# A decoder block with a product-key expert layer on one core: nine list tiles a block in place of ten

## The chip, the cores and the metric

The kernel runs on one core of a Trainium2 chip. The metric is the device time of one execution in microseconds (us). Before the change the median of three runs is 1511.7 us (1509.28 to 1516.68).

## The reference

One decoder layer for 1024 tokens of width 1024: two mixing branches with an output projection, then an expert layer (PEER), then a final norm. All matrices are float32. What matters here is the expert layer:

```python
q = jnp.einsum('btd,dq->btq', h, w_q).reshape(B, T, H, 2, PEER_DQ // 2)
s1 = jnp.einsum('bthc,kc->bthk', q[..., 0, :], keys1)
s2 = jnp.einsum('bthc,kc->bthk', q[..., 1, :], keys2)
v1, i1 = lax.top_k(s1, K)          # K = 16, H = 8 heads, 128 keys
v2, i2 = lax.top_k(s2, K)
cand = (v1[..., :, None] + v2[..., None, :]).reshape(B, T, H, K * K)
cidx = (i1[..., :, None] * PEER_NKEYS + i2[..., None, :]).reshape(B, T, H, K * K)
top_s, pos = lax.top_k(cand, K)
idx = jnp.take_along_axis(cidx, pos, axis=-1)
g = jax.nn.softmax(top_s, axis=-1)
...
u = expert_down[ii]
a = jax.nn.gelu(jnp.einsum('pd,ped->pe', xx, u), approximate=False)
vv = expert_up[ii]
return jnp.einsum('pe,ped->pd', gg * a, vv)
```

Each token picks 16 of 16384 experts in each of 8 heads. The scores are large (the inputs scale the query weights and both key tables by 8), so most of the 16 softmax gates underflow to zero in float32.

## The kernel before, in words

The 1024 tokens are handled as two halves of 512 and eight blocks of 128 (blocks 0 to 3 and 4 to 7). For each half a chain of weight groups is streamed (`stream`, L1180): a 128x512 weight tile is loaded by SP, split into a high and a low float32r part by ScalarE (L1190) and VectorE (L1191), and multiplied in three passes (L178 to L186). The last groups of a half are the output projection (`w_out_part`) and the four query groups `w_q(0)` to `w_q(3)`. After each of those, `s_part` computes the key scores, `tops` takes the best 8 (L197, L198), and `rank(q)` writes the expert indices of each token's best expert for two heads into a table (L1548).

**Directs and lists.** For each token and head the best expert always counts. These eight "direct" tiles a block (128 tokens, one head) are gathered by the index table, one 128x2048 row pair a token (or two gathers of 128x1024, where the buffer is a pair), dotted with the tokens (L518), and added with a diagonal weight matrix (L586, plain float32). The experts of rank 2 to 8 count only where their gate is at least the smallest normal float32. They are packed into one list a block. `pack_half` counts the entries of each block (`cnt`), and the list is processed in tiles of 128 entries: `peer_E` builds a one-hot matrix (L691, L692), `entry_list` moves the entries' indices and gates with two matmuls (L531, L532), gathers 128 rows of both expert tables (L509), and `entry_dot` fetches the tokens' activations with four matmuls (L561, L562) and dots them in two halves (L563). Blocks 0 and 1 gather the tokens' activations instead (L547) and dot them at once (L568). In the first stage the weighted rows are added in float32r with a split (L595, L596, then four matmuls at L603, L604); in the second stage in plain float32 (two matmuls at L586). The number of list tiles a block is the constant `NT` (L43); entries past the end of a list give tiles whose rows have weight zero, and they are gathered and added all the same.

Heads whose eighth gate is not zero (`flags`) leave the lists and go through one "rare" list for each half (`NTR`, six tiles each).

**The order.** `peer_stream` (L738) writes the order of all tiles out: the rare list of the first half, the lists of blocks 0 to 3 (their directs were summed earlier by `direct_rows`), some directs of blocks 5, 6, 7 and 4 (`EARLY`), and then, as a second stage with its own pools, the remaining directs (`LATER`), the lists of blocks 4 to 7, the second rare list, and the final rows. The first stage is pumped by `step()` in between the weight groups of the second half; directs are only listed once their `rank(q)` has been issued (`topped`). The buffers of gathered rows are used in a fixed ring (`RING`, `RING9`), and up to `AH` tiles are gathered ahead. A scheduler with a model of the machine then sets each engine's order, so that one constant can move many instructions.

**The general pass.** `peer_rest` (L898) adds up by how much each count exceeds its capacity, `caps` (L905, `NT * 128` entries a block). If the sum is above zero, a loop over all eight blocks and 128 selections each redoes the whole layer (L913 on). Otherwise it is skipped. It follows the last tile.

Of the kernel before, what the change touches and what calls it, by code (L numbers as in the profile page):

```python
# [39 lines left out]
GRP = {b: (g, i) for g, bs in enumerate(GROUPS) for i, b in enumerate(bs)}  # L40
ROW0 = (0, 16, 24, 32, 40, 44, 48, 52, 56)
NC_ = 64
NT = 10  # L43
NTR = (6, 6)
EB = 2
WS = 4
# [31 lines left out]
def block_kernel(ctx: ExitStack, tc: tile.TileContext, x, xT, cT, w_ada, b_ada, b_adaT, n1T, w_inp, w_alr,  # L78
# [37 lines left out]
    def load_const(name, src, shape, pool=None):  # L116
# [8 lines left out]

    ebase = const.tile([P, NT], F32, name="ebase")
    nc.gpsimd.iota(ebase, pattern=[[P, NT]], base=0, channel_multiplier=0,
                   allow_small_or_imprecise_dtypes=True)
# [350 lines left out]
    def load_block(pl, b, h2):  # L479
        hh = hl = None  # L480
        if pl["own"] or b not in HRB:
            if h2 is None:
                h2 = load_h2(b)
            ph = use[turns[0] % len(use)]["ph"]
            turns[0] += 1
            hh = ph.tile([P, D], F32R, name="hh", tag="hh")
            hl = ph.tile([P, D], F32R, name="hl", tag="hl")
            nc.scalar.activation(hh, h2, AF.Identity)
            nc.vector.tensor_tensor(hl, h2, hh.bitcast(F32), op=OP.subtract)
        if b in onchip:  # L490
            return b, hh, hl, *onchip[b]
        n = ncs_of[b]
        th = pl["pw"].tile([P, 3 * NCS + 2], F32R, name="thl")[:, :3 * n + 2]
        tl = pl["pw"].tile([P, 2 * NCS], F32R, name="tll")[:, :2 * n]
        nc.scalar.dma_start(th.bitcast(F32), ts_d[b][:, :3 * n + 2])
        nc.scalar.dma_start(tl.bitcast(F32), ts_d[b][:, 3 * n + 2:])
        return b, hh, hl, th, tl
# [177 lines left out]
    def peer_prep(pl, b, h2):  # L675
        blk = load_block(pl, b, h2)
        mid = pl["pw"].tile([P, NT], F32, name="mid")
        hw = pl["pw"].tile([P, 2], F32, name="hw")
# [6 lines left out]
    def peer_E(pl, pb, j):  # L685
        blk, mid, hw = pb
        eb = pl["eb"]
        n = min(eb, NT - j) * P
        ea = pl["pq"].tile([P, eb * P], F32, name="ea", bufs=1)
# [48 lines left out]
    def peer_stream():  # L738
        last = PH + NT
        todo, opens, closes, runs = [], set(), set(), set()  # L740
# [157 lines left out]
    def peer_rest(pl, pg_):  # L898
# [5 lines left out]
        morei = pc.tile([1, 1], I32, name="morei")  # L904
        caps = [NT * P] * NBLK + [t * P for t in NTR] + [P] * NG  # L905
        for i, c in enumerate(caps):
# [758 lines left out]
```

## Time and profile before

| | |
|---|---|
| median of 3 runs | 1511.7 us (1509.28 to 1516.68) |
| profiled execution: its own time | 1513.0 us |
| profiled execution: span of the trace | 1511.3 us |
| PE busy | 1386.3 us (92%) |
| VectorE (DVE) busy | 1116.6 us (74%) |
| ScalarE (ACT) busy | 751.4 us (50%) |
| GpSimd (POOL) busy | 331.5 us (22%) |
| moved by DMA | 360 MB, mean 238 GB/s |

The own time lies 1.7 us over the span. Busy time of PE is the sum of matmul records that overlap each other, so it can be close to the span without PE being at its peak. POOL issues all gathers, in order. The first stage of the expert tiles runs from about 795 us, beside the second half's weight groups, the hand-over to the second stage takes from about 1224 to 1345 us, and the second stage's lists run to the end.

### The profile page before, as it was taken

To read this page: it belongs to the slowest core of one execution; us is meant where nothing else is said; L and a number is where in the kernel's file an instruction comes from. 1 tells how busy PE (TensorE), PEld (TensorE's weight loads), DVE (VectorE), ACT (ScalarE), POOL (GpSimd) and SP (SyncE) were. 2 spreads that over 40 slices of the span, in tenths; PEclk is the share of its full clock that TensorE was granted. 3 is DMA by queue.
4 is the path that set the end of the run, shared out by engine and by line. 5 is a ranking of instruction groups with operands and counts; after the bars stand their busy time and mean duration, and the time that the engine had idled before them with its cause. 6 is when DMAs were issued, how large, how long until landed. Compare 5 with 4: busy or idle time off the path is not lost.

```text
span 1511.3 us, 20046 instructions
## 1 busy us (share of the span) xinstructions
PE 1386.3 (92%) x6076; PEld 1060.7 (70%) x6076; DVE 1116.6 (74%) x3189; ACT 751.4 (50%) x1659; POOL 331.5 (22%) x302
## 2 busy tenths in 40 slices
PE   3999999999997999989899999998989999679985
PEld 2778777888776877668677878876778775246542
DVE  6483867434567779987789678779898786898883
ACT  4463333332445545474445675556555555455542
POOL 0000002000000121602433132311111145554430
PEclk7899999999999999999999999999999999889998
DMA  9553644233358545856776698976878669899964
GB/s 317 182 198 103 202 147 140 98 105 118 132 196 281 197 162 175 299 185 206 257 264 238 217 349 312 343 267 226 299 285 278 247 263 360 332 406 390 356 252 149
DMA packets 126167, 360.24 MB, mean 238 GB/s; under 512 B 15625, under 2 KB 25097, under 8 KB 115170
## 3 DMA queue, kind: packets, MB, share of 16 engines
q0 software_dynamic: 35952, 175.39, 31.5%
q1 hardware_dynamic: 70272, 132.15, 25.8%
q10 hardware_dynamic: 19826, 51.34, 9.6%
q8 instruction: 49, 0.80, 0.2%
q14 instruction: 68, 0.56, 0.1%
HBM read 334.60 MB, written 24.23 MB: 237 GB/s over the span
## 4 chain that ended last, share of the span: by engine, by line
PE 61%; DMA 16%; DVE 15%; issue 4%; ACT 3%; POOL 1%; ACTq 0%; SPq 0%; DVEq 0%; POOLq 0%
PE mm L178 10%; PE mm L179 10%; PE mm L181 10%; PE acc L586 5%; PE mm L184 4%; PE mm L185 4%; PE mm L186 4%; DMA uv<-in_tab_dram,dix 3%; DMA uv<-in_tab_dram,ix 2%; DMA wada<-in_w_ada_dram 2%; DVE wl L1191 2%; PE hps L561 2%; PE hps L562 1%; DMA wt<-in_w_outp_dram 1%; DVE ti L198 1%
## 5 line engine op out<-in xcount | busy, mean ns | idle before, releaser
L1190 ACT ACTIVATE wh<-wt 128x512 fp32r<-128x512 f32 x368 | 228.3, 628 | 309.2 <-PE mm L179 115.9
L1191 DVE TENSOR_TENSOR wl<-wt,wh 128x512 fp32r<-128x512 f32 x368 | 248.9, 686 | 154.3 <-ACT wh L1190 81.0
L178 PE MATMUL mm<-wh,hTh 128*128 128x512 f32 x672 | 266.9, 399 | 2.3 <-ACT wh L1190 2.3
L179 PE MATMUL mm<-wh,hTl 128*128 128x512 f32 x672 | 265.9, 398 | 0.0
L181 PE MATMUL mm<-wl,hTh 128*128 128x512 f32 x672 | 209.2, 397 | 0.0
L178 PEld LDWEIGHTS mm<-wh,hTh 128*128 128x128 f32 x672 | 128.3, 191 | 34.8 <-ACT wh L1190 4.5
L179 PEld LDWEIGHTS mm<-wh,hTl 128*128 128x128 f32 x672 | 128.3, 191 | 27.9 <-issue 0.9
L181 PEld LDWEIGHTS mm<-wl,hTh 128*128 128x128 f32 x672 | 126.6, 189 | 28.0 <-DVE wl L1191 0.7
L509 POOL DMA_INDIRECT uv<-in_tab_dram,ix x70 | 78.2, 1118 | 274.6 <-ACT ix L540 135.9
L184 PE MATMUL mm<-wh,hTh 128*128 128x512 f32 x224 | 91.5, 417 | 15.6 <-ACT hTh L1144 6.4
L178 PE MATMUL mm<-hTh,wh 128*128 128x512 f32 x240 | 95.9, 400 | 0.0
L179 PE MATMUL mm<-hTl,wh 128*128 128x512 f32 x240 | 95.5, 398 | 0.0
L185 PE MATMUL mm<-wl,hTh 128*128 128x512 f32 x224 | 89.7, 400 | 0.0
L186 PE MATMUL mm<-wh,hTl 128*128 128x512 f32 x224 | 89.0, 400 | 0.0
L184 PE MATMUL mm<-hTh,wh 128*128 128x256 f32 (+1 forms) x208 | 72.1, 350 | 11.4 <-ACT vt L1235 5.5
L561 PE MATMUL hps<-hh,E 128*128 128x512 f32 x144 | 71.8, 500 | 11.0 <-DVE uv L563 8.9
L563 DVE SCALAR_TENSOR_TENSOR uv<-uv,hps 128x512 f32<-128x512 f32 x100 | 66.8, 682 | 17.9 <-PE hps L562 9.4
L181 PE MATMUL mm<-hTh,wl 128*128 128x512 f32 x240 | 74.0, 401 | 0.0
L185 PE MATMUL mm<-hTl,wh 128*128 128x256 f32 (+1 forms) x208 | 70.8, 342 | 2.5 <-DVE hTl L170 2.5
L596 DVE SCALAR_TENSOR_TENSOR vl<-uv,r,vh 128x512 fp32r<-128x512 f32 x88 | 63.7, 746 | 11.1 <-PE acc L604 5.9
L186 PE MATMUL mm<-hTh,wl 128*128 128x256 f32 (+1 forms) x208 | 69.8, 342 | 1.2 <-DVE wl L1191 1.0
L712 POOL DMA_INDIRECT uvd<-in_down_dram,dix x32 | 37.1, 1159 | 139.9 <-DVE ts L351 45.7
(977 smaller groups left out, 3021.0 us busy)
## 6 DMA issues: line engine op xcount, KB each, us to landing
wt<-in_w_inp_dram SPq DMA_DIRECT2D x224, 256.0 KB, 3.1
wt<-in_w_qp_dram SPq DMA_DIRECT2D x80, 256.0 KB, 3.2
wada<-in_w_ada_dram SPq DMA_DIRECT2D x32, 512.0 KB, 4.3
wt<-in_w_outp_dram SPq DMA_DIRECT2D x64, 256.0 KB, 3.6
wada<-in_w_ada_dram SPq DMA_DIRECT2D x32, 256.0 KB, 6.0
s_d<-so ACTq DMA_DIRECT2D x32, 256.0 KB, 3.5
h2l<-h_d ACTq DMA_DIRECT2D x13, 512.0 KB, 7.0
xr<-in_x_dram ACTq DMA_DIRECT2D x8, 512.0 KB
```

What stands on the lines that cost most here:

```text
L178: nc.tensor.matmul(ps, lh, rh, start=False, stop=False)
L179: nc.tensor.matmul(ps, *((lh, rl) if feat else (ll, rh)), start=False, stop=False)
L181: nc.tensor.matmul(ps, *((ll, rh) if feat else (lh, rl)), start=False, stop=False)
L184: nc.tensor.matmul(ps, lh, rh, start=first, stop=False)
L185: nc.tensor.matmul(ps, lh, rl, start=False, stop=False)
L186: return nc.tensor.matmul(ps, ll, rh, start=False, stop=last).ins
L509: nc.gpsimd.indirect_dma_start(out=dst[:], out_offset=None, in_=src, in_offset=off)
L561: nc.tensor.matmul(hps, Ej, hh[:, sl], start=True, stop=False)
L563: nc.vector.scalar_tensor_tensor(uv[0][:, sl], uv[0][:, sl], 1.0, hps, op0=OP.mult, op1=OP.mult, accum_out=r[:, 2 + n:3 + n])
L586: nc.tensor.matmul(acc[:, sl], W, v[:, sl], start=first, stop=last)
L1190: nc.scalar.activation(wh, wt, AF.Identity)
L1191: nc.vector.tensor_tensor(wl, wt, wh.bitcast(F32), op=OP.subtract)
```

## The change

The constant `NT` is 9 in place of 10, so that each block's list has nine tiles, 1152 entries of capacity in place of 1280, and blocks with more entries go through the general pass.

```diff
 NC_ = 64
-NT = 10
+NT = 9
 NTR = (6, 6)
```

Through `NT` it changes the width of `ebase` and `mid` (L126, L677), the last direct or list index `last` (L739), the width of the last one-hot matrix (L688) and `caps` (L905). PE's order is the same up to the first list tile of block 0, and differs from there on.

The first place is POOL's order at the hand-over from the lists of block 3 to the directs (`dix_0_136` and `dix_1_137` are the index tables that `rank(0)` and `rank(1)` of the second half write; `ix` is a list's index; `fs` belongs to the finish of a block). Before:

```order
L509 DMA uv<-in_tab_dram,ix 128x2048
L509 DMA uv<-in_tab_dram,dix_0_136 128x2048
L509 DMA uvu<-in_down_dram,ix 128x1024
L509 DMA uvv<-in_up_dram,ix 128x1024
L509 DMA uvu<-in_down_dram,dix_0_136 128x1024
L509 DMA uvv<-in_up_dram,dix_0_136 128x1024
L166 TENSOR_TENSOR fs<-fs,mhalf 128x1
L509 DMA uv<-in_tab_dram,dix_1_137 128x2048
```

After the change:

```order
L509 DMA uv<-in_tab_dram,ix 128x2048 x4
L509 DMA uvu<-in_down_dram,dix_0_136 128x1024
L509 DMA uvv<-in_up_dram,dix_0_136 128x1024
L509 DMA uv<-in_tab_dram,dix_0_136 128x2048 x2
L166 TENSOR_TENSOR fs<-fs,mhalf 128x1
L509 DMA uvu<-in_down_dram,dix_1_137 128x1024
L509 DMA uvv<-in_up_dram,dix_1_137 128x1024
```

All list gathers now stand ahead of the first direct gather, and three direct gathers in place of two stand ahead of block 3's finish.

The second place is VectorE's order ahead of `rank(3)` (L1548, `dix_3_139`), which frees the last quarter of the directs; L518 is the dot of one direct. Before:

```order
L518 SCALAR_TENSOR_TENSOR uvu,rd<-uvu,h2l 128x1024
L518 SCALAR_TENSOR_TENSOR uv,rd<-uv,h2l 128x1024
L198 MAX_INDEX ti<-tv,so 128x8 x6
L345 TENSOR_TENSOR cand<-tv 128x8x8
L345 TENSOR_TENSOR cand<-tv 128x8x4 x3
L1548 SCALAR_TENSOR_TENSOR dix_3_139<-ti 128x8
```

After the change:

```order
L198 MAX_INDEX ti<-tv,so 128x8 x4
L345 TENSOR_TENSOR cand<-tv 128x8x8
L345 TENSOR_TENSOR cand<-tv 128x8x4 x3
L518 SCALAR_TENSOR_TENSOR uv,rd<-uv,h2l 128x1024
L1548 SCALAR_TENSOR_TENSOR dix_3_139<-ti 128x8
```

One dot now stands directly ahead of the index write. Over the whole order 22 of the 32 direct dots stand ahead of it, where 20 did; in POOL's order 23 direct gathers stand ahead of the first that needs it, as before.

## Rows read from the trace of the kernel before

**Rows 1.** The page: span, and the chain that ended last, by engine.

```profile
span 1511.3 us, 20046 instructions
...
PE 61%; DMA 16%; DVE 15%; issue 4%; ACT 3%; POOL 1%; ACTq 0%; SPq 0%; DVEq 0%; POOLq 0%
```

**Rows 2.** Busy time by window: PE, PEld, DVE, ACT, POOL; PEclk; DMA share; GB/s.

```profile
795.00:900.00 105.00, 101.58 (x447) 82.43 (x446) 84.47 (x223) 66.48 (x155) 30.39 (x26) 0.98 0.74 262
900.00:1000.00 100.00, 97.43 (x463) 80.09 (x462) 78.03 (x200) 62.74 (x147) 28.20 (x25) 1.00 0.89 327
1000.00:1130.00 130.00, 116.47 (x520) 91.94 (x519) 112.52 (x260) 76.23 (x165) 19.34 (x18) 0.93 0.75 265
1130.00:1244.00 114.00, 109.40 (x570) 89.56 (x570) 93.06 (x356) 63.50 (x135) 30.04 (x27) 0.99 0.72 257
...
1350.00:1440.00 90.00, 88.93 (x302) 52.02 (x301) 73.46 (x309) 51.43 (x170) 40.93 (x42) 1.00 0.97 373
```

**Rows 3.** The chain that ended last, second stage: start, length, what.

```profile
1364.45 1.72 PE acc L586 x4
...
1367.55 1.72 PE acc L586 x4
...
1408.13 1.73 PE acc L586 x4
```

**Rows 4.** PE in order of time, one list tile of the second stage.

```profile
1390.71 1.88 PE L586 MATMUL acc<-uvv,W 128*128 128x512 f32 x4
1392.03 0.80 PE L561 MATMUL hps<-hh,E 128*128 128x512 f32 x1
1392.67 0.39 PE L562 MATMUL hps<-hl,E 128*128 128x512 f32 x1
1392.90 0.24 PE L531 MATMUL tps<-th,E 128*128 128x170 f32 x1
...
1393.60 1.88 PE L586 MATMUL acc<-uv,W 128*128 128x512 f32 x4
```

**Rows 5.** PE in order of time, a stretch of weight matmuls without expert tiles.

```profile
319.75 0.39 PE L185 MATMUL mm<-wl,hTh 128*128 128x512 f32 x1
...
322.93 0.39 PE L186 MATMUL mm<-wh,hTl 128*128 128x512 f32 x1
```

**Rows 6.** Groups of VectorE instructions, 795 to 1244 us: busy, mean ns, idle before.

```profile
L596 DVE SCALAR_TENSOR_TENSOR vl<-uv,r,vh 128x512 fp32r<-128x512 f32 x88 | 63.7, 746 | 11.1 <-PE acc L604 5.9 <-ACT vh L595 4.0 <-PE hps L562 0.7
L563 DVE SCALAR_TENSOR_TENSOR uv<-uv,hps 128x512 f32<-128x512 f32 x48 | 32.1, 681 | 10.5 <-DMA uv<-in_tab_dram,ix 8.1 <-PE hps L562 2.2
L568 DVE SCALAR_TENSOR_TENSOR uv<-uv,hr 128x1024 f32<-128x1024 f32 x20 | 24.4, 1221 | 12.6 <-DMA uv<-in_tab_dram,ix 9.4 <-DMA hr<-h_d,ix 3.3
L692 DVE TENSOR_SCALAR E<-ea,hw 128x128 fp32r<-128x128 f32 x44 | 12.4, 281 | 1.4 <-PE tps L532 1.1 <-ACT ea L691 0.4
L563 DVE DVE_READ_ACCUMULATOR uv<-uv,hps 128x1 f32 x48 | 3.9, 82 | 0.0
```

**Rows 7.** POOL in order of time at the hand-over, with the idle time before.

```profile
1193.32 0.95 POOL L509 DMA_INDIRECT uvv<-in_up_dram,dix  x1 [0.30 <-issue]
1222.21 0.56 POOL L166 TENSOR_TENSOR fs<-fs,mhalf 128x1 f32<-128x1 f32 x1 [27.95 <-DVE fs L165]
1223.94 1.45 POOL L509 DMA_INDIRECT uv<-in_tab_dram,dix  x1 [1.17 <-DVE dix L1548]
...
1300.45 0.94 POOL L509 DMA_INDIRECT uvu<-in_down_dram,dix  x1 [13.22 <-DVE ts L351]
```

**Rows 8.** Groups of PE instructions, 795 to 1244 us.

```profile
L604 PE MATMUL acc<-vl,e 128*128 128x512 f32 x92 | 38.2, 415 | 2.6 <-DVE vl L596 2.6
...
L561 PE MATMUL hps<-hh,E 128*128 128x512 f32 x52 | 21.9, 421 | 4.9 <-DVE uv L563 4.7 <-ACT ts__9424 L534 0.2
...
L531 PE MATMUL tps<-thl,E 128*128 128x170 f32 (+1 forms) x45 | 11.5, 258 | 1.1 <-DVE uv L563 1.1
```

**Rows 9.** The chain that ended last: a gather of the hand-over, and the last block's finish.

```profile
1239.74 12.95 DMA uv<-in_tab_dram,dix
...
1475.82 10.16 DMA yrv<-x_d
...
1494.27 3.71 PE acc L586 x8
```

## The prediction

> **What bounds the kernel now.** I read the page first. The chain that ended last lies 61% on PE, 16% on DMA and 15% on VectorE [rows 1], so no single engine's busy time gives the answer, and what a list tile is worth has to be read in each stage. The change removes eight list tiles, the tenth of each block: four in the first stage (blocks 0 to 3, beside the weight groups of the second half) and four in the second stage (blocks 4 to 7).
>
> The second view is busy time by window [rows 2]. From 1350 to 1440 us PE is busy 88.93 of 90 us and the DMA engines carry 0.97 of their time at 373 GB/s. Two resources are full at once. In the first stage (795 to 1244 us, four windows) PE's records cover 90 to 97%, VectorE's 78 to 87%, and DMA has room except between 900 and 1000 us (0.89). There a list tile costs something, but it is not plain on which engine.
>
> The third view is the chain in the second stage [rows 3]: it stays on PE, and the additions of successive list tiles start 1364.45, 1367.55, ..., 1408.13 us. That is 15 tiles in 43.68 us, 2.91 us a tile. PE in order of time shows one tile from inside [rows 4]: from the addition at 1390.71 to the next at 1393.60 us, with the additions, the activation matmuls and the index matmuls end to end. 1.72 us of it are the two float32 additions [rows 3].
>
> **Second stage: minus 11.6 us.** Each of the four removed tiles takes with it one step of this train: 4 x 2.91 = 11.6 us. It makes no difference here which of the two full resources sets the pace, since the tile takes both loads away: PE's 2.9 us, and 1.05 MB of gathers, which at 373 GB/s last 2.8 us [rows 2]. VectorE and ScalarE lie beside it (VectorE 73 of 90 us), and nothing is added. The one-hot matrices are built in pairs, so nine tiles need five of them as ten do: nothing is saved there, and nothing hangs on it. The lower end is three tiles, 8.7 us: at the end of the program the last block's tiles wait for the finishes of other blocks and a load of 10.16 us [rows 9], and one tile of block 7 may be in the shadow of that.
>
> **First stage: minus 9.5 us.** Here a list tile stands among weight matmuls. Without expert tiles these start 0.227 us apart: from 319.75 to 322.93 us there are 14 steps in 3.18 us [rows 5]. A list tile has four float32r additions and two narrow index matmuls, which I count together as one, so 5 x 0.227 = 1.1 us in blocks 0 and 1; blocks 2 and 3 add four activation matmuls, 9 x 0.227 = 2.0 us. Four tiles: 2 x 1.1 + 2 x 2.0 = 6.3 us (6.4 unrounded). That is the lower end, if PE alone paces the stage.
>
> The other end is VectorE, whose instructions are counted in full since they do not overlap [rows 6]: two splits of 0.746, the one-hot of 0.281, and either one dot of 1.221 (blocks 0 and 1, sum 2.99) or two of 0.681 with their 0.082 read (blocks 2 and 3, sum 3.30). Four tiles: 2 x 2.99 + 2 x 3.30 = 12.6 us. The chain holds both engines, so I take the middle, 9.5 us. The edit adds no work, so I see no loss in the stage itself; the ways in which the gain could be lost stand among the rivals.
>
> The records of the matmuls that go away last longer than the step: 0.415 us for an addition, 0.421 for an activation matmul, 0.258 for an index matmul [rows 8]. Charged at that, the four tiles would be 12.1 us of PE and the whole sum 23.7 if PE paced. But the starts in [rows 5] are 0.227 us apart while each record lasts 0.39, so the records overlap and the step is the price. The Trainium skill says the same as a warning, on the page "Perfetto Trace Analysis", section "Identifying the Most-Contended Engine": matmul busy time is no good measure of how near TensorE is to its peak, since pipelined instructions overlap in the trace. By that rule, the trace agrees: 6.4 and not 12.1 us is PE's end.
>
> **The hand-over between them.** Here the order moves most. Before, POOL issues two direct gathers by 1193 us, then stands 27.95 us behind block 3's finish, and goes on at 1223.94 us, when VectorE has written the second index table; the last quarter of the directs starts at 1300.45 us, 13.22 us after POOL was free [rows 7]. After the change the list of block 3 ends earlier, its finish stands ahead of the second index table, and three direct gathers are issued early in place of two. That third gather is no gain I count, since 23 direct gathers stand ahead of the last index table before and after. Against it, VectorE has 22 dots, not 20, ahead of that table, and each waits for its gather. Before, 21 direct gathers were issued between 1223.94 and 1300.45 us, 3.64 us each, so two more dots could cost 2 x 3.64 = 7.3 us, and the same amount is the most that a shorter wait there may give. I take zero between these and keep both for the range. Work that comes earlier by the first stage's 9.5 us brings the whole hand-over forward: the index tables depend on the weight groups, which PE reaches earlier.
>
> **Sum.** 9.5 + 11.6 = 21.1 us. The profiled execution took 1513.0 us of its own (span 1511.3), so 1491.9; it lies 1.3 us above the median of the three runs, so the median should come to 1490.6, in round figures **1491 us**, 1.4% less. A measurement of this kernel tells about 0.5%, 7.6 us, from no change: faster means below 1504.1.
>
> **Rivals.**
>
> *The first stage hides its tiles.* The tiles are pumped by the weight groups' steps, and if those are paced by weights that arrive late or by VectorE work that stays, four tiles less shorten nothing. For it: PE's share falls to 90% between 1000 and 1130 us, with DMA at 0.75 and VectorE at 87% [rows 2]. Against it: in the other three windows PE is at 96% or so. Then only the second stage counts: 1511.7 - 11.6 = 1500.
>
> *The hand-over gives it back.* VectorE is in order, and its 22 dots delay the last index table by 7.3 us against the rest: 1490.6 + 7.3 = 1498. For it: the 13.22 us wait of [rows 7] is of this kind. Against it: the gathers that the dots wait for start earlier too. Both rivals together give 1507, no measurable change.
>
> *The general pass is entered: slower.* It stands behind the last tile and starts as soon as one block's count exceeds 9 x 128 = 1152; the point from which it decides is the 1153rd entry. Its loop runs 8 x 128 = 1024 times with a gather of 1.05 MB each. At 373 GB/s [rows 2] that is 2.8 us a pass, 2.9 ms in all; with a gather waited for each time, 12.95 us [rows 9], some 13 ms. The kernel would take 4400 to 15000 us. The trace has no counts, but the inputs are fixed: evaluating the reference's routing in float32 for its seed 0, the eight blocks have 1138, 1095, 1101, 1095, 1117, 1067, 1129 and 1107 entries whose gate is a normal float32. The largest leaves 14 places free. The same reckoning gives 634 and 475 entries in the rare lists (capacity 768) and at most 65 flagged heads (capacity 128). Gates at the threshold move with rounding, but entries spread over some 87 units of score difference, about 13 in each, so rounding moves a few at most.
>
> *The change does less than it says.* That would be the padding tiles costing nothing before. Against it: the order shows the removed tiles' gathers and matmuls gone, and the trace shows tiles in a steady train with no shorter ones among them [rows 3].
>
> *More than forecast.* The first stage at VectorE's end and 7.3 us off the hand-over: 1490.6 - 3.1 - 7.3 = 1480.
>
> **Chances.** Forecast 0.60; first stage hidden 0.16; hand-over gives back 0.10; more than forecast 0.04; first stage and hand-over together (1507) 0.06; general pass 0.04. Faster by over 0.5% are the first four less 0.02 for a hidden first stage that also hides a tile at the end: 0.88. Within 0.5%: 0.06 + 0.02 = 0.08. Slower: 0.04, all of it the general pass. The range is 1480 to 1503 us: from the larger gain to 3 us above the first rival (one tile of the end in the shadow); outside lie the combined rivals, the general pass and tails, together under 0.2.
>
> **What would show it.** Right: 42 list tiles in the second stage at an unchanged 2.9 us, so that from the last quarter's gathers to the end there are 11 to 12 us less; the first gather by the second index table (1223.94 us before) 6 to 13 us earlier; no row of the general pass. The first stage is wrong if 1223.94 has moved by less than 5 us; the hand-over is wrong if the distance from there to the last quarter (76.5 us before) has changed by more than 5 us; the second stage is wrong if the step of a tile is no longer 2.9 us, which would mean that two full resources were not the pace. Any row of the loop behind the last tile makes the whole forecast wrong.

## The result, and the profile after

The change takes **1477.1 us** (median of four runs, 1473.6 to 1480.3) where the kernel before took 1513.5 us beside it (four runs, 1509.3 to 1516.7): a ratio of 0.976 with a 95% interval of 0.973 to 0.980. That is 36.4 us less; the forecast was 21 us less, and the time lies 3 us under the range of 1480 to 1503 us. The same kernel, compared again on two further occasions, took 1484.0 and 1482.1 us, 24.6 and 26.2 us less than before (experiments 3 and 7); both times lie inside the range. So the mean of three comparisons is about 29 us, and the first is the largest of them.

The profiled execution took 1480.3 us of its own, 1478.6 us of span. The page of the changed kernel, its span and its busy time by engine (no row of the loop behind the last tile stands on it; busy time is the time in which at least one record of the engine runs, each moment counted once, and not the sum of the records):

```profile
span 1478.6 us, 19700 instructions
...
PE 1364.5 (92%) x6004; PEld 1049.7 (71%) x6004; DVE 1095.6 (74%) x3109; ACT 737.4 (50%) x1609; POOL 313.6 (21%) x288
```

Busy time by window, the same stretches as in [rows 2] (PE, PEld, VectorE, ScalarE, POOL; PE's granted clock; share and GB/s of the DMA engines):

```profile
795.00:900.00 105.00, 101.41 (x445) 82.11 (x444) 85.32 (x224) 66.01 (x153) 30.41 (x26) 0.98 0.74 262
900.00:1000.00 100.00, 95.03 (x446) 78.19 (x445) 71.86 (x184) 58.03 (x133) 25.34 (x22) 0.98 0.82 300
1000.00:1130.00 130.00, 120.38 (x522) 92.48 (x520) 114.99 (x269) 79.49 (x172) 20.77 (x20) 0.95 0.76 271
1130.00:1244.00 114.00, 110.13 (x580) 88.67 (x579) 91.25 (x334) 60.39 (x133) 28.49 (x24) 1.00 0.79 286
1350.00:1440.00 90.00, 89.89 (x304) 52.46 (x303) 76.12 (x306) 49.19 (x162) 36.56 (x38) 1.00 0.91 346
```

Against [rows 2], PE is about as full in the first stage as it was (427 of 449 us busy, 425 before), and in the steady stretch of the second stage it is still full while the DMA share fell from 0.97 to 0.91. PE in order of time, an addition of the second stage and the one eleven tiles later:

```profile
1366.85 1.98 PE L586 MATMUL acc<-uv,W 128*128 128x512 f32 x4
...
1398.56 1.88 PE L586 MATMUL acc<-uvv,W 128*128 128x512 f32 x4
```

Eleven steps in 31.71 us are 2.88 us a tile, as in [rows 3] (2.91). The hand-over on POOL, which answers to [rows 7]:

```profile
1176.54 1.31 POOL L509 DMA_INDIRECT uvu<-in_down_dram,dix  x1 [19.87 <-DVE dix L1548]
...
1185.77 0.64 POOL L166 TENSOR_TENSOR fs<-fs,mhalf 128x1 f32<-128x1 f32 x1 [0.44 <-DVE fs L165]
1208.49 0.98 POOL L509 DMA_INDIRECT uvu<-in_down_dram,dix  x1 [22.08 <-DVE ts L351]
...
1287.64 0.98 POOL L509 DMA_INDIRECT uvu<-in_down_dram,dix  x1 [11.02 <-DVE dix L1548]
```

POOL no longer stands 27.95 us behind block 3's finish; it stands 19.87 us in front of the first gather by the first index table and 22.08 us in front of the first by the second. The first gather by the second index table comes at 1208.49 us (1223.94 before, 15.5 us earlier), the last quarter 79.15 us later (76.51 before). From that last quarter to the end there are 190.96 us, where there were 210.85. At the end, the chain of the changed kernel runs over the last block's tiles:

```profile
1450.22 1.98 PE acc L586 x4
...
1453.13 1.72 PE acc L586 x4
...
1455.78 1.72 PE acc L586 x4
...
1463.09 3.71 PE acc L586 x8
```

The load of 10.16 us that stood in the chain before [rows 9], 35 us ahead of the end, is not in it; the chain of the changed kernel can be followed back 36 us, to 1442.82 us, and has no transfer in it.

### The profile page after: what moved, and what is told of

Same layout as the page of the kernel before. It is cut to its first block, busy times and chain, and to the rows that moved or that the text cites. A ratio compares the mean times of both kernels' runs of the same rounds, so it can differ in the third digit from the quotient of the medians.

```text
span 1478.6 us, 19700 instructions
## 1 busy us (share of the span) xinstructions
PE 1364.5 (92%) x6004; PEld 1049.7 (71%) x6004; DVE 1095.6 (74%) x3109; ACT 737.4 (50%) x1609; POOL 313.6 (21%) x288
## 5 line engine op out<-in xcount | busy, mean ns | idle before, releaser
L561 PE MATMUL hps<-hh,E 128*128 128x512 f32 x132 | 65.6, 498 | 6.9 <-DVE uv L563 4.2
L181 PE MATMUL mm<-hTh,wl 128*128 128x512 f32 x240 | 70.7, 395 | 0.0
```

The costliest lines, as they stand in the source:

```text
L181: nc.tensor.matmul(ps, *((ll, rh) if feat else (lh, rl)), start=False, stop=False)
L561: nc.tensor.matmul(hps, Ej, hh[:, sl], start=True, stop=False)
```

## The experiments

Every experiment was timed beside the kernel before on its own chip, so effects are given against that; chips differ, and the kernel before had medians of 1505.6 to 1513.5 us.

### 1. One stage at a time

Nine tiles in one stage and ten in the other. The edit against the kernel before, cut (the tuple is turned round for the other kernel, and the order of the tiles takes each block's own number):

```diff
 NT = 10
+NTB = (9, 9, 9, 9, 10, 10, 10, 10, 10, 10)
...
-        n = min(eb, NT - j) * P
+        n = min(eb, NTB[pb[0][0]] - j) * P
...
-        caps = [NT * P] * NBLK + [t * P for t in NTR] + [P] * NG
+        caps = [t * P for t in NTB[:NBLK]] + [t * P for t in NTR] + [P] * NG
```

Nine in the first stage:

> Nine list tiles in blocks 0 to 3 and ten in blocks 4 to 7, so only the first stage loses tiles. The second index table moved by 15 us and the last quarter of the directs by 13 us in the trace of the change. If the last 8 us of the gain are the place of the last block's buffers in the ring (theory RING), they are gained here too, since this kernel's 128 tiles also put the last final row into a plain 2048-wide buffer that is free early: about 13 + 7 = 20 us faster than before. If the gain at the end belongs to the tiles removed in the second stage (theory TILES), 13 us. If the first stage is worth what was forecast, 9.5 us, or 16 with RING.

Nine in the second stage:

> Ten list tiles in blocks 0 to 3 and nine in blocks 4 to 7, so only the second stage loses tiles. RING: 11.6 us for four tiles at 2.9 us and 7 us for the last load, about 19 us faster than before. TILES: the whole 20 us by which the stretch from the last quarter of the directs to the end became shorter. Forecast as it stood: 11.6 us.

The kernel before took 1506.2 us there. Nine in the first stage took 1494.0 us (ratio 0.990, 0.986 to 0.994), nine in the second 1490.0 us (0.989, 0.985 to 0.993). Each half is worth something, 12.2 and 16.2 us by the medians (9 to 22 and 11 to 23 by the intervals), and neither hides its tiles.

### 2. The ring of buffers and the last load

Since the load of [rows 9] had gone from the chain, one theory was that the gain came from where the ring of buffers stood at the end, not from the tiles. The ring was turned in the changed kernel, and in the kernel before (there by one place, so that the last block's load takes another buffer):

```diff
-            return (use[0]["pt"], b4, use[1]["pt"])[RING9[k % len(RING9)]]
+            return (use[0]["pt"], b4, use[1]["pt"])[RING9[(k + 8) % len(RING9)]]
```

> The change, with the ring of the second stage turned by 8 places so that the last final row falls into the same kind of buffer pair as before the change; its x2 load then again waits for the finish of block 5 on VectorE. RING: 6 to 8 us slower than the change, about 29 us faster than before, and a DMA wait of some 10 us for x2 back in the chain of the last 40 us. TILES: as the change, within 3 us.

> The kernel before (ten tiles everywhere), with the ring of the second stage turned by one place so that the last final row falls into the kind of buffer that it has after the change. RING: 6 to 8 us faster than before, and no x2 wait in the chain of the last 40 us. TILES: no change within 3 us.

The changed kernel with its ring turned took 1477.8 us (0.981, 0.977 to 0.986), so 28 us less than before, as the two halves of experiment 1 add up to. In its trace the load does not stand in the chain either, so it does not bring the wait back and tells only that the turn costs nothing. The kernel before with its ring turned by one took 1511.0 us (1.002, 1.000 to 1.005); the load has left its chain, and nothing was gained. But another transfer has come into the chain at the same place, 32 us ahead of the end:

```profile
1469.28 10.45 DMA uv<-in_tab_dram,ix
```

The kernel with nine tiles in the first stage and ten in the second (experiment 1) has such a gather too, 9.06 us long, 35 us ahead of the end; in the five traces of the table further down with nine tiles in the second stage no transfer stands in the last 35 us of the chain. So the load itself is no part of the gain, but a late transfer goes with the tenth tile of the second stage, and this experiment does not take that wait away.

### 3. What paces the first stage, and the change once more

The change again, the change with VectorE work added, and the change with PE work added, in each of the 42 list tiles of the first stage:

> The change itself once more, as the reference of the runs beside it: 0.976 of the kernel before, some 36 us.

```diff
-        nc.vector.tensor_scalar(e2, iota[:, int(lane0(b)):int(lane0(b)) + P], ts_[:, 3 * n:3 * n + 1], None, op0=OP.is_equal)
+        for _ in range(1 if own else 4):
+            nc.vector.tensor_scalar(e2, iota[:, int(lane0(b)):int(lane0(b)) + P], ts_[:, 3 * n:3 * n + 1], None, op0=OP.is_equal)
```

> The change, with the entry's one-hot of 0.28 us on VectorE written four times instead of once in each of the 42 list tiles of the first stage: 126 more VectorE instructions, 35 us of VectorE, nothing on another engine, same output. Theory VECTOR (VectorE paces a list tile of the first stage): 28 to 35 us slower than the change, all of it ahead of the second index table. Theory PE (PE paces): under 10 us slower. Both in part: 10 to 28.

```diff
+        for _ in range(0 if own else 12):
+            nc.tensor.matmul(tps, Ej, th, start=True, stop=True)
         nc.tensor.matmul(tps, Ej, th, start=True, stop=False)
```

> The change, with the index matmul of 128x170 done 12 more times in each of the 42 list tiles of the first stage: 504 more matmuls of about 0.075 us, 38 us of PE, nothing on another engine, same output. Theory VECTOR: under 10 us slower than the change. Theory PE: 30 to 38 us slower, all of it ahead of the second index table. Both in part: 10 to 30.

The change took 1484.0 us (0.983, 0.979 to 0.988; before 1508.5). The VectorE work made it 1488.6, only 4.7 us longer: 126 instructions of 0.28 us, 35 us by their records, which raise VectorE's busy time by 26.7 us (from 1094.7 to 1121.4). The PE work made it 1521.2, 37.3 us longer. The expectation put it at 0.075 us a matmul, 38 us in all; the trace shows more. Twelve added matmuls and the first that is the tile's own:

```profile
857.17 1.47 PE L532 MATMUL tps<-thl,E 128*128 128x170 f32 x12
858.48 0.27 PE L533 MATMUL tps<-thl,E 128*128 128x170 f32 x1
```

Twelve steps in 1.31 us are 0.109 us each, so that the 504 added come to some 54 us; PE's busy time rises by 53.3 us (from 1358.6 to 1411.9). Busy time by window, 795 to 1130 us (columns as above), first of the changed kernel on this chip:

```profile
795.00:1130.00 335.00, 313.11 (x1409) 250.51 (x1408) 270.56 (x670) 201.64 (x453) 75.65 (x67) 0.97 0.77 274
```

then with VectorE work added:

```profile
795.00:1130.00 335.00, 313.46 (x1430) 252.63 (x1429) 287.42 (x750) 204.30 (x446) 66.33 (x62) 0.96 0.75 271
```

and with PE work added:

```profile
795.00:1130.00 335.00, 327.24 (x1700) 273.96 (x1699) 241.79 (x614) 182.57 (x410) 64.49 (x61) 0.99 0.70 248
```

VectorE took 16.9 us more in this stretch, and PE, at 313 us, got as much done. With more matmuls PE fills the stretch and everything else in it becomes less. So PE paces the first stage, though not one for one: of some 54 us 37.3 were paid, and 15 us went into time in which PE had stood (from the first list gather to the second stage's first list addition it stands 50.1 us in the changed kernel and 35.3 us here). VectorE has room: of 27 to 35 us 4.7 were paid.

### 4. What paces the second stage

Three kernels leave work out of its list tiles. The first gathers only the down rows and uses them for both purposes (the up rows are left out):

```diff
-    def gather(ul, ix):
+    def gather(ul, ix, half=False):
...
+        if half:
+            nc.gpsimd.indirect_dma_start(out=uv[0][:], out_offset=None, in_=down, in_offset=off)
+            return [uv[0], uv[0]]
```

> The change, with the 42 list tiles of the second stage gathering only the first expert table's rows and using them in place of the second table's too: the up rows of these tiles are left out of the computation. PE and VectorE keep their work, DMA loses 42 times 0.5 MB. Theory STREAM (the gathers from the second index table to the end are one stream that paces the second stage, so that a list tile is worth 15/4 = 3.75 us there): 21 MB less at some 0.37 MB a us, 30 us or more faster than the change. Theory TRAIN (PE's step of 2.9 us paces and the rest of the 15 us is waiting around it): under 10 us faster, the step of the tiles still 2.9 us.

The second adds only the first half of each row in 35 of the 42 tiles (the second halves are left out):

```diff
-            for n in range(2):
+            for n in range(halves):
...
-                add_rows(wv, accs[b], fst, lst)
+                add_rows(wv, accs[b], fst, lst, 1 if len(use) > 1 and PH <= j < last and not fst and not lst else 2)
```

> The change, but 35 of the 42 list tiles of the second stage add only the first 512 columns of their rows (one float32 matmul of 0.86 us in place of two); the second halves are left out of the sum. If TensorE paces the second stage, some 35 x 0.86 = 30 us less than the change, so about 55 to 65 us less than before. If the gathers' stream paces it, as much as the change: 25 to 36 us less than before. If both are close to full, something between, with TensorE's busy share falling in the last quarter.

The third does both:

> The change, but list tiles of the second stage gather only the down rows (used for both purposes; the up rows are left out) and 35 of the 42 add only the first half of the row (the second halves are left out): the two loads that one half-way kernel each took away, taken away together. If TensorE and the gathers' stream were both full, so that taking one load away left the other as the pace, the two together give much more than each alone: VectorE would be next (73 of 90 us in the steady stretch before), so a fifth off 122 us, some 20 to 25 us less than the change. If a tile's step is set by something else (a chain of waits from gather to dot to addition, VectorE's order, the loads of the final rows), it gives no more than the kernel that halves the additions alone, some 5 to 10 us less than the change.

Half the gathers took 1490.8 us (0.989, 0.985 to 0.993), 6.8 us longer than the change beside it (1484.0). Half the additions took 1468.5 us (0.974, 0.971 to 0.977; before 1505.6), 37 us less than before, so some 11 us under the change, not 30. Both took 1472.4 us (0.976, 0.972 to 0.980), 9.7 us less than the change beside it (1482.1). Halving the gathers leaves the step of the steady train as it is; PE in order of time in that kernel, an addition and the one twelve tiles later (its line numbers are three higher):

```profile
1361.00 1.88 PE L589 MATMUL acc<-uv,W 128*128 128x512 f32 x4
...
1395.48 1.88 PE L589 MATMUL acc<-uv,W 128*128 128x512 f32 x4
```

Twelve steps in 34.48 us are 2.87 us a tile. Nothing is gained behind the train either, where a load of final rows stands in the chain; why this kernel is longer is not shown:

```profile
1434.83 6.20 DMA yr<-x_d
```

With half the additions the steps shorten to 2.0 us, and then the chain goes over to waits for gathers and to VectorE's dots:

```profile
1345.86 0.86 PE acc L586 x2
1347.86 0.86 PE acc L586 x2
1349.95 0.86 PE acc L586 x2
1351.96 0.86 PE acc L586 x2
...
1357.61 8.81 DMA uvv<-in_up_dram,ix
...
1375.47 0.62 DVE uv L563 x2
```

With both halved, the busy time from 1340 to 1380 us is:

```profile
1340.00:1380.00 40.00, 39.02 (x142) 23.59 (x141) 39.15 (x185) 26.79 (x96) 15.95 (x17) 1.00 0.72 244
```

VectorE is at 39.15 of 40 us there, the next engine to be full. So in the changed kernel PE sets the 2.9 us step, with waits for gathers and VectorE a little behind it: taking PE's load away gives back only the distance to the next (11 of 30 us). A removed tile takes all three loads away, and experiment 5 shows what a whole tile is worth.

### 5. Prices from many tiles

Thirteen tiles a block in one stage, nine in the other; all that are added are padding. The edit is that of experiment 1 with `NT = 13`.

> Thirteen list tiles in each of blocks 0 to 3 and nine in blocks 4 to 7, so twelve padding tiles more than before in the first stage and four fewer in the second. With 2.91 us for a tile of the second stage and the forecast's middle of 2.4 us for one of the first: 28.5 - 11.6 = 17 us more than before. If only TensorE's own steps count (1.6 us a tile): 8 us more. If VectorE's sum counts (3.15 us): 26 us more. If the first traces are right as they stand (3.05 and 3.7 us): 22 us more. If the nine-tile kernels owe their gain to an arrangement of the order and not to the tiles, no such line holds, and the time may lie anywhere.

> Nine list tiles in blocks 0 to 3 and thirteen in each of blocks 4 to 7: four padding tiles fewer than before in the first stage and twelve more in the second. With the forecast's prices (2.4 and 2.91 us): 34.9 - 9.5 = 25 us more than before. With the first stage at TensorE's steps alone (1.6 us): 28 us more; at VectorE's sum (3.15 us): 22 us more. With the prices of the first traces (3.05 and 3.7 us): 32 us more. Together with the kernel of thirteen tiles in the first stage it gives both prices by two equations.

Thirteen in the second stage took 1527.6 us (1.014, 1.010 to 1.018; before 1505.6). With the first stage's 12.2 us off (experiment 1), twelve tiles cost 22.0 + 12.2 = 34.2 us, 2.85 us each (2.3 to 3.3 by its interval). Against the change on the same chip (26.2 us less than before, experiment 7) sixteen tiles cost 48.2 us, 3.0 each. Thirteen in the first stage took 1552.1 us (1.030, 1.027 to 1.034), far more than any price of a tile foretold: 46.5 + 16.2 = 63 us for twelve, 5.2 each. There the lists outlast the weight groups that pump them: block 3's finish comes 2 us behind the fourth index table, where with ten tiles it stands 71 to 78 us ahead of it. POOL in order of time of that kernel, its last list gathers (its line numbers are one higher):

```profile
1276.65 0.94 POOL L510 DMA_INDIRECT uvu<-in_down_dram,ix  x1 [15.80 <-ACT ix L541]
1283.78 0.94 POOL L510 DMA_INDIRECT uv<-in_tab_dram,ix  x1 [4.95 <-ACT ix L541]
1288.94 1.08 POOL L510 DMA_INDIRECT uvu<-in_down_dram,ix  x1 [2.90 <-ACT ix L541]
```

They come when the first direct gathers by an index table (1253.3 us) are already out, and POOL waits for each list's index. So this kernel tells nothing of the price below ten tiles, and the two-equation reckoning that its expectation offered does not hold.

### 6. Fewer padding tiles still

The rare lists have 634 and 475 entries by the reference, so five and four tiles hold them (640 and 512 places).

```diff
-NTR = (6, 6)
+NTR = (5, 4)
```

> The change, with rare lists of five and four tiles in place of six and six (634 and 475 entries by the reference, so 640 and 512 places): one padding tile fewer in the first stage and two in the second. By the forecast's prices 2.4 + 5.8 = 8 us less than the change, by those of the first traces 3.05 + 7.4 = 10 us less: some 33 to 46 us less than before. If a list overflows, the general pass runs and the time is above 4000 us.

It took 1461.6 us (0.970, 0.967 to 0.973), 44 us less than before, and so beats the change. Since that is more than its three tiles' price, the parts were run alone, with `(5, 6)` and `(6, 4)`, and the whole again:

> The change, with the first rare list at five tiles in place of six (634 entries in 640 places) and the second unchanged: one padding tile fewer in the first stage. By the forecast's price 2.4 us less than the change, by TensorE's steps alone 1.6 us, by VectorE's sum 3.3 us: 27 to 30 us less than before. If the first tile of the stage holds up everything behind it (the trace of the kernel with both rare lists cut has the fourth index table 20 us earlier than the change), 10 us or more less than the change: over 35 us less than before.

> The change, with the second rare list at four tiles in place of six (475 entries in 512 places) and the first unchanged: two padding tiles fewer at the end. By 2.91 us a tile 5.8 us less than the change, about 31 to 34 us less than before. If the first stage's tile is what the kernel with both lists cut gains from, and the end is held by the final rows, 0 to 3 us less than the change.

> Rare lists of five and four tiles once more, beside the two halves. If the parts add up, its gain against the change is the sum of those of the two; the first comparison gave 44 us less than before (ratio 0.9701). If that comparison was a lucky draw: 33 to 36 us less than before.

One tile fewer in the first stage took 1467.2 us (0.973, 0.970 to 0.976; before 1507.7), 40.5 us less than before; two fewer at the end took 1474.1 us (0.977, 0.974 to 0.980), 33.6 less; both took **1458.5 us** (0.967, 0.964 to 0.970), 49.2 less. Against the change (26.2 us less than before in experiment 7, the nearest in number of runs) that is 14, 7 and 23 us; against the mean of its three comparisons (29) it is 11, 5 and 20. The two at the end are worth 2.3 to 3.7 us each, about a step. The one of the first stage is worth 11 to 14 us, where PE's own steps for a tile of this stage are 1.1 to 2.0 us by the prediction's count. Where these come from is seen in what PE waits for. Waits of PE from 795 to 1250 us (who waits for whom, us in total, times, longest) in the changed kernel of experiment 7:

```profile
PE acc L603 <- ACT vh L595: 4.7, 5, 1.4
PE sps L1422 <- ACT us L1227: 3.6, 1, 3.6
PE aux L1563 <- issue: 2.9, 1, 2.9
```

and in the kernel with one tile fewer:

```profile
PE hps L561 <- DVE uv L563: 2.5, 4, 1.5
PE mm L178 <- ACT wh L1190: 2.5, 2, 2.1
...
PE acc L603 <- ACT vh L595: 1.2, 2, 1.0
```

The busy time of the same stretch, first of the changed kernel:

```profile
795.00:1250.00 455.00, 429.53 (x1987) 341.67 (x1986) 366.70 (x1058) 267.61 (x591) 104.85 (x92) 0.98 0.77 274
```

then with one tile fewer:

```profile
795.00:1250.00 455.00, 439.22 (x2051) 351.19 (x2049) 372.79 (x1080) 275.88 (x601) 106.79 (x99) 0.98 0.78 285
```

PE stands 25.5 us of 455 in the one and 15.8 us in the other, 9.7 us less; 3.6 us of that is the wait for `us` (L1227) and 3.5 us that for the split of list rows (L595). One pair of traces overstates how sure this is: in the three traces of the change PE stands 22.1, 29.5 and 25.5 us of these 455, in the three with five tiles in the first rare list 15.8, 18.6 and 18.4, so on average 8 us less. One tile fewer shifts every later tile against the weight groups, and the order of the whole stage comes out anew. Which part of the new order takes the standstills away was not tried.

### 7. The change a third time, and eight tiles

> The change once more, beside the kernel before on this chip. The first comparison gave 36 us less, the second on another chip 25 us less; the kernels that do one half each add to 28, and the prices from the kernels with thirteen tiles give 34. If the forecast's sum (21) is right and the first comparison was a lucky draw, near 21 to 25; if the measured prices are right, 28 to 36.

The change took 1482.1 us (0.984, 0.981 to 0.987; before 1508.3), 26.2 us less.

```diff
-NT = 9
+NT = 8
```

> Eight list tiles a block: 1024 places, and by the reference every block has more entries (1067 to 1138), so the general pass must run. The prediction's third rival priced it at 2.9 to 13 ms: between 4400 and 15000 us, and rows of the loop behind the last tile. If the time is about 1450 us, the counts are smaller than reckoned and the general pass was never near.

It took 12852 us, so the general pass runs. From its page: the span, PE's granted clock in tenths over 40 slices, the loop's dot and its gather:

```profile
span 12850.1 us, 84121 instructions
...
PEclk9999755555555555555555555555555555555555
...
L943 DVE SCALAR_TENSOR_TENSOR uv<-uv,h2l 128x1024 f32<-128x1024 f32 x1024 | 1255.0, 1226 | 5890.8 <-DMA uv<-in_tab_dram,gix 5890.8
L509 POOL DMA_INDIRECT uv<-in_tab_dram,gix x1024 | 967.0, 944 | 10304.7 <-DVE gkc L948 10304.7
```

With some 1450 us for the rest, the 1024 passes take about 11.1 us each. Every gather waits for the pass before it (10304.7 us of idle time on POOL), so of the two bounds of the prediction, 2.8 and 12.95 us a pass, the second is the nearer. Some block has more than 1024 entries, as the counts of the prediction say; that none has more than 1152 is seen in the change, which has no row of the loop.

## Why the prediction was wrong, and what in it was right

The traces of eight runs, cut at the first addition of a second-stage list tile, show which term was off. Times in us, the first counted from the first list gather of the first stage; beside each the time in which PE is busy:

| tiles in the first and second stage | to the first list addition of the second stage | PE busy | from there to the end | PE busy |
|---|---|---|---|---|
| 10 and 10: before, ring turned | 557.5, 556.4 | 509.4, 508.3 | 158.0, 156.7 | 137.9, 137.9 |
| 10 and 9 (experiment 1) | 549.4 | 502.5 | 142.9 | 125.8 |
| 9 and 10 (experiment 1) | 545.2 | 497.5 | 152.8 | 137.8 |
| 9 and 9: the change, three traces | 543.9, 549.4, 547.4 | 498.7, 499.3, 501.3 | 138.3, 138.2, 138.2 | 125.0, 124.9, 124.9 |
| 9 and 9: the change, ring turned | 535.4 | 493.4 | 146.1 | 129.3 |

Two of them in their rows, first the kernel before, then the change (columns as in [rows 2]):

```profile
795.76:1353.28 557.52, 509.39 (x2232) 388.34 (x2232) 453.59 (x1440) 321.08 (x747) 164.87 (x144) 0.95 0.81 294
1353.28:1511.30 158.02, 137.87 (x445) 76.90 (x443) 114.77 (x425) 72.70 (x235) 57.17 (x57) 0.97 0.77 290
```

```profile
796.38:1340.28 543.90, 498.70 (x2203) 380.01 (x2202) 441.58 (x1395) 312.59 (x719) 153.67 (x136) 0.97 0.80 293
1340.28:1478.60 138.32, 125.04 (x405) 70.62 (x403) 106.29 (x388) 66.90 (x213) 48.47 (x51) 0.97 0.78 295
```

The last row of the table parts its 681.5 us differently and is left out of the means. From the two traces with ten and ten to the three of the change, the first stretch is 10.0 us shorter and the second 19.1, together 29.2 us. PE's busy time falls by 9.1 + 12.9 = 22.0 us, the time in which PE stands by 1.0 + 6.2 = 7.2 us.

**The step that failed: the waits were put at nothing.** The sum, 21.1 us, prices removed work, and PE's busy time fell by 22.0. Of the standstills around this work the prediction says "I see no loss in the stage itself", "I take zero between these" at the hand-over, and at the end it knows only a loss ("three tiles, 8.7 us"). They shrank by 7.2 us, 6.2 of it behind the first list addition of the second stage. The table shows with which tiles they went. Nine tiles in the first stage take 4.6 us off the second stretch, whether the second stage has ten or nine, and most of this is standing (19.5 to 15.0 us with ten, 17.1 to 13.3 with nine). Nine tiles in the second stage take 14.5 us off it, 12 to 13 of them PE's work. So a tile less in the first stage also made PE wait less in the second. Which stop of the train that is was not tried. It is not the late transfer of experiment 2, which the kernel with nine and ten still has; that one can belong to the 2 us of standing that go with the second stage's own tiles.

**First stage: the size near, by luck.** The prediction took "the middle" of PE's 6.3 us and VectorE's 12.6, 9.5, because "the chain holds both engines"; the first stretch became 10.0 us shorter. Experiment 3 shows that VectorE does not pace this stage, so of the two ends PE's was the sound one and the middle has no ground. Nor can the first stretch be booked to these four tiles alone: the kernel with ten and nine loses no tile ahead of that point and still reaches it 7.5 us earlier than before. The traces hold one thing that differs there and that the prediction left out, PE's granted clock. Between these two points PE has the lower of its two levels (1.2 GHz in place of 2.4, 0.50 in the row below) for 51 us in both traces with ten and ten, for 37 us in all three of the change, for 37 us with ten and nine and for 30 us with nine and ten. Before one of these drops, from 1020 to 1034 us, PE was busy 10.30 of 14 us. The row of that drop in the kernel before, and two matmuls in it:

```profile
1034.20:1041.00 6.80, 5.93 (x18) 4.38 (x19) 6.80 (x18) 3.64 (x9) 1.94 (x2) 0.50 0.25 75
```

```profile
1037.32 0.63 PE L604 MATMUL acc<-vl,e 128*128 128x512 f32 x1
1037.74 0.63 PE L603 MATMUL acc<-vh,e 128*128 128x512 f32 x1
```

Matmuls of 512 columns start 0.42 us apart there, in place of 0.227. By these rows 14 us less at the lower level are worth at most 6.4 us, an estimate that takes PE as busy with such matmuls all the time. No run varied the clock by itself, so how much of the gain it is stays open; it can account for the 4 us by which PE's busy time fell more than the steps of the removed matmuls (6.4 + 11.6 = 18.0 us).

Two readings of the prediction are wrong without moving the sum. Its rounded terms 2 x 1.1 + 2 x 2.0 make 6.2, not 6.3. And VectorE's records do overlap; in the kernel before:

```profile
849.72 1.41 DVE L596 SCALAR_TENSOR_TENSOR vl<-uv,r,vh 128x512 fp32r<-128x512 f32 x2
851.05 0.27 DVE L549 SCALAR_TENSOR_TENSOR jk<-ts__7193,slot 128x56 f32<-128x56 f32 x1
```

Two splits take 1.33 us by the starts, where two records of 0.746 make 1.49. On the other side the count leaves out three short instructions of each tile (L537, L549, L552; about 0.2 us each by the starts), so that VectorE's end stays near what was put. For its warning the Trainium skill, on the page and in the section that the prediction names, gives as the reason that pipelined PE instructions "look smaller in the trace"; that the records overlap is read from [rows 5], not from that page.

**Second stage: the mechanism right.** The step in the steady train is unchanged, 2.88 us, as foretold; tiles added cost 2.85 to 3.0 us each (experiment 5); and four tiles fewer took 12 to 13 us of PE's work, where the prediction put 4 x 2.91 = 11.6.

**The rest is the first comparison.** The traces give 29.2 us and the two repeats 24.6 and 26.2, where the prediction put 21. The first comparison had 36.4; its interval (31 to 41 us) lies above that of the third (20 to 29). The three traces of the same changed kernel reach the first list gather between 789.4 and 796.4 us, so a difference of some us between executions needs no change at all. That the time fell under the range hangs on that draw, since the repeats lie inside it; what made the first comparison the largest stays open.

**Rivals.** *The first stage hides its tiles* fell: these tiles alone gave 12.2 us (experiment 1). *The hand-over gives it back* fell too: the distance from the second index table's gather to the last quarter changed by 2.6 us, within the 5 that were allowed. *More than forecast* is nearest in its number, 1480, but not by its mechanism, which was VectorE's end and 7.3 us of the hand-over. *The change does less than it says* fell with the second-stage tiles of experiment 5, all padding, which cost their full step. *The general pass* was not entered; its price is 11.1 us a pass.

**What would show it.** From the last quarter's gathers to the end there were to be 11 to 12 us less, and there were 19.9 less, so this sign spoke against the forecast while the step of a tile stood at 2.9 us: what went beyond it were waits. The second index table's gather was to come 6 to 13 us earlier, and came 15.5 earlier. The later marker moved less: VectorE's write of the fourth index table comes 498.3 us behind the first list gather with ten tiles in the first stage (mean of three traces), 493.1 with nine (five traces). So part of a gain that shows at the second table may be given back on the way to the fourth; but the two traces with ten and ten alone lie 10 us apart there, so neither is a good marker.

## What to carry to other kernels

The price of a step in a steady train, read from starts and not from busy records, held for removing it as for adding it, even where several resources were nearly full. Where tiles are threaded into other work, ask with a dose on each engine which one paces, read the dose itself from starts too, and give the range room for the standstills of that engine, further down the program as well: here 7 of 29 us were waits that went with the tiles, most of them in the stage behind. Look at the granted clock of both traces before a difference is booked to the edit. Padding is worth counting in every list: here five and four tiles for the rare lists gave more than half as much again as the change, at a smaller margin (634 entries in 640 places), and a list that overflows costs 11 ms.

## What the runs showed of the hardware

A narrow index matmul of 170 columns steps 0.109 us in a run of twelve (rows of experiment 3), about half of the 0.227 us of a 512-column matmul [rows 5], though it has a third of the columns; its record lasts 0.27 us. In the loop of the general pass, where PE has no matmul at all (none from 5000 to 5100 us), the granted clock falls to its lower level, 1.2 GHz (0.5 in the row of experiment 7), and ScalarE loads a table of its functions in each of the 1024 passes, 1.28 us each:

```profile
L945 ACT ACT_TABLE_LOAD x1024 | 1313.8, 1283 | 2526.3 <-PEq L933 2526.2
```
